# Raw weight halves in the common pool of split weights, and a longer price for loads in the planner

## Chip, core and metric

One NeuronCore of a Trainium2 chip runs the whole program. The metric is the time of one execution on the device in microseconds (us); the median of several runs is compared.

## What is computed

Two layers of an encoder on 256 tokens of width 1024, in float32. Each layer is a half-step SwiGLU, a mixer of two groups of heads, and a second half-step SwiGLU; a norm follows at the end.

```python
def reference(x, ...):
    for l in range(DEPTH):
        x = x + 0.5 * swiglu(rms_norm(x, ffn1_norm[l]), ffn1_w_gate[l], ffn1_w_up[l], ffn1_w_down[l])
        h = rms_norm(x, mix_norm[l])
        proj = h @ w_in[l]
        y_rwkv = rwkv7_group(proj[..., :RWKV_IN], ...)   # delta rule over tokens
        y_ret = retnet_group(proj[..., RWKV_IN:])        # chunk-causal retention
        mixed = jnp.concatenate([y_rwkv, y_ret], axis=-1)
        x = x + mixed @ w_out[l]
        x = x + 0.5 * swiglu(rms_norm(x, ffn2_norm[l]), ffn2_w_gate[l], ffn2_w_up[l], ffn2_w_down[l])
    return rms_norm(x, final_norm)
```

Nearly all the arithmetic is the matrix products with the weights: 166 pieces of 128 x 2048 numbers (1 MB), each of which is used by both token tiles.

## The kernel before

**Tiles and weights.** The 256 tokens are two tiles of 128. A weight piece is handled in two halves of 128 x 1024 (512 KB). `half` loads such a half once, as float32, and splits it into a high part (a ScalarE copy to fp32r, `whi`) and a low part (a VectorE subtraction, `wlo`). `mm3` then makes three matmuls of 512 columns for each 128 x 512 of weights: high by high, high by low, low by high. So a half feeds 6 matmuls for each token tile, 12 in all. The first four halves (EARLY) are loaded and split in two cuts of 512 columns.

**Feed-forward.** `ffn` goes through 11 blocks of 256 columns of gate and up (tile `gu`), makes hh with a ScalarE Silu and a VectorE product, transposes hh on TensorE (`tr`), splits the transposed block into `ht` (ScalarE, then VectorE), and multiplies with the rows of the down weights into `acc`. `norm_T` transposes x and splits it into `parts`.

**Mixer.** `mix` follows PLAN. The delta rule needs the inverse of small triangular blocks; for that, `inverse` sends them through DRAM and back on SyncE's queue (el to d twice, d to mx, mi to d, d to misc, for each tile and layer). `merge` and `chain` are small matmuls that depend on each other.

**Order.** Nothing is emitted as it is written. The calls are recorded as nodes (`record`), priced (`price`), and ordered by a simulated list schedule (`simulate`); `schedule` tries the eight GUIDES with up to SERIES = 4 refinements each and keeps the order with the earliest simulated end. `emit` writes the instructions of all engines in that order, and each engine then runs its own queue in order, waiting at semaphores. The halves' loads are tied to each other in program order (`in_turn`), all on SyncE's queue. A node that needs a new buffer may only start, in the simulation, when enough places of that kind are free.

**Places.** Split halves live in a pool of 22 "wide" places of 4 KB a partition, two for each half, from the first write to the last read. Raw halves live in a ring of three (NRAW, line 31) inside the tile `base`, outside the pool; a load can only be issued when the VectorE split of the half three before has read its buffer. In a profile, `base<-in_w` is such a load, `wide<-base` a ScalarE split, `wide<-base,wide` a VectorE split. All instructions are emitted from one line (L542), so the groups of the profile are told apart by their tiles.

**Price of a load.** A load occupies the simulated fabric for its bytes divided by 290 (in ns), and lands 2000 ns after that.

Of the kernel before, what the change touches and what calls it, by code (L numbers as in the profile page):

```python
# [12 lines left out]
F32 = mybir.dt.float32  # L13
F32R = mybir.dt.float32r
# [6 lines left out]
D = 1024  # L21
S = 256
P = 128
# [4 lines left out]
DEPTH = 2  # L28
RW = 512
HD = 64  # L30
NRAW = 3
XG = (0, 8, 16)
XCUT = (2, 1)
WARM = 1
# [2 lines left out]
FIRST = 2  # L37
# [17 lines left out]
PIECES = 33 + 13 + 4 + 33  # L55
# [6 lines left out]
NBASE = 3072  # L62
# [5 lines left out]
    return ap.unsqueeze(2).to_broadcast(shape)  # L68


PLACES = {"slot": (43, 2048), "wide": (22, 4096), "bank": (8, 2048)}
GUIDES = (5, 7, 10, 14, 20, 25, 30, 40)
SERIES = 4
TURN = -1.0
ENGINES = {"tensor": 0, "vector": 1, "scalar": 2, "gpsimd": 3, "sync": 4}


# [105 lines left out]
class Plan:  # L183
# [178 lines left out]
    def simulate(self, prio):  # L362
# [14 lines left out]
        fabric = 0.0  # L377
# [9 lines left out]
        while done < total:  # L387
            if not events:
                raise Stuck(f"stuck at {t}, {done} of {total}: " + ", ".join(
                    f"{nodes[r[0][1]].ops[0].call} {nodes[r[0][1]].ops[0].args[0].buf.name}" for r in ready if r))  # L390
            t = heapq.heappop(events)
            while events and events[0] <= t:
                heapq.heappop(events)
            while pending and pending[0][0] <= t:
                ft, _, b = heapq.heappop(pending)
                places[b.space].append((ft, b.place))
            for e in range(5):
                if free_at[e] > t:
                    continue
                w, r = waiting[e], ready[e]  # L400
                while w and w[0][0] <= t:
                    i = heapq.heappop(w)[1]
                    heapq.heappush(r, (-prio[i], i))
                held = []
                while r:
                    item = heapq.heappop(r)
                    n = nodes[item[1]]
                    ok = True
                    new = [b for b in n.touched if b.place is None]
                    if new:  # L410
                        wants = {}
                        for b in new:
                            wants[b.space] = wants.get(b.space, 0) + 1
                        if e == 0 and n.dur > 115:
                            wants["bank"] += 1
                        ok = all(len(places[k]) >= v for k, v in wants.items())
                    if ok:
                        break
                    held.append(item)
                else:  # L420
                    n = None
                for h in held:
                    heapq.heappush(r, h)
                if n is None:
                    continue
                for b in new:
                    pool = places[b.space]
                    j = min(range(len(pool)), key=lambda k: pool[k][0])
                    b.place = pool.pop(j)[1]
                    low[b.space] = min(low.get(b.space, 99), len(pool))  # L430
                form = n.ops[0].form
                extra = 0.0
                if e == 0:
                    if state[0] != form:
                        extra = 95.0
                        state[0] = form
                elif e == 2 and form in ("s", "t"):
                    if state[2] != form:
                        extra = 1280.0
                        state[2] = form  # L440
                n.start = t
                dur = n.dur + extra
                n.real = dur
                free_at[e] = t + dur
                heapq.heappush(events, t + dur)
                shift = extra
                if form == "dma":
                    size = n.ops[0].n
                    begin = max(t, fabric)
                    fabric = begin + size / 290.0  # L450
                    land = fabric + 2000.0
                    shift = land - t
                done += 1
                fin = t + dur
                for s, lag in n.succs:
                    a = t + 60 if lag is TURN else t + shift + lag
                    if a > avail[s.i]:
                        avail[s.i] = a
                    need[s.i] -= 1
                    if not need[s.i]:  # L460
                        heapq.heappush(waiting[s.eng], (avail[s.i], s.i))
                        heapq.heappush(events, max(avail[s.i], t))
                if form == "dma":
                    fin = t + shift
                    n.land = shift
                elif e == 0:
                    fin = t + shift + n.ops[-1].at + n.ops[-1].late
                end = max(end, fin)
                for b in n.touched:
                    b.last = max(b.last, fin + 60)  # L470
                    left[b.i] -= 1
                    if not left[b.i]:
                        heapq.heappush(pending, (b.last, b.i, b))
                        heapq.heappush(events, b.last)
# [15 lines left out]
    def schedule(self):  # L490
# [3 lines left out]
        way, n = self.tails(), len(self.nodes)  # L494
        best = None
        for guide in GUIDES:
            prio = [w + guide * (n - i) * 1e5 / n for i, w in enumerate(way)]
            for k in range(SERIES):
                try:
                    end = self.simulate(prio)  # L500
                except Stuck:
                    break
                if best is None or end < best[0]:
                    best = (end, prio)
# [5 lines left out]
    def emit(self, ctx, tc):  # L510
        nc = tc.nc
        sp = ctx.enter_context(tc.tile_pool(name="sbuf", bufs=1))
        pp = ctx.enter_context(tc.tile_pool(name="psum", bufs=1, space=PSUM))
        dp = ctx.enter_context(tc.tile_pool(name="dram", bufs=1, space=bass.MemoryType.DRAM))
        for b in self.bufs:
            if b.space == "fixed":
                b.real = sp.tile(b.shape, b.dt, name=b.name, tag=b.name)
        pools = {"slot": sp, "bank": pp, "dram": dp}
        wide = [sp.tile([P, 1024], F32R, name=f"wide{i}", tag=f"wide{i}") for i in range(PLACES["wide"][0])]

        def place(b):
            size, tag = b.elems, f"{b.name}{b.i}"
            if b.space == "wide":
                b.real = wide[b.place]
                return
            if b.space in PLACES:
                size, tag = PLACES[b.space][1] // SIZE[b.dt], f"{b.space}{b.place}"
            v = pools[b.space].tile([b.shape[0], size], b.dt, name=f"{b.name}_{b.i}", tag=tag, bufs=1)[:, :b.elems]
# [16 lines left out]
VERBOSE = False  # L545


class Trunk:
    def __init__(self, plan, x, w, vecs, lora, fgain, consts, out):
# [1 line left out]
        self.vecs_d, self.lora_d = vecs, lora  # L551
        self.A = self.plan = plan
        self.nc = nc = plan
        base = plan.fixed([P, NBASE + (2 + NRAW) * D], F32, "base")
        parts = plan.fixed([P, NT, 2, KD, P], F32R, "parts")
        self.x, self.xh, self.xl = [], [], []
        for t in range(NT):
# [4 lines left out]
        self.c = base[:, :NBASE]  # L562
        nc.scalar.dma_start(self.c[:, C_ID:C_ID + P], consts[:, C_ID:C_ID + P])
        self.load_x(0)
        self.raw = base[:, NBASE + 2 * D:].rearrange("p (n i) -> p n i", n=NRAW)
        self.nraw = 0
        self.consts_d = consts
        self.scan = self.c[:, C_SCAN:C_SCAN + 256].bitcast(BF16)
        nc.vector.memset(self.scan, 1.0)
# [44 lines left out]
    def half(self, i, h):  # L614

        if (i, h) not in self.wq:
            nc = self.nc
            raw = self.raw[:, self.nraw % NRAW]
            self.nraw += 1
            cut = 512 if 2 * i + h < EARLY else 1024  # L620
            for c in range(0, 1024, cut):
                nc.sync.dma_start(raw[:, c:c + cut], self.w_d[i][:, 1024 * h + c:1024 * h + c + cut])
                nc.in_turn()
            kind = sum(i % PIECES >= b for b in (33, 33 + FIRST, 46, 50)) % 4
            hi = self.A.get([P, 1024], "whi", F32R, kind)
            lo = self.A.get([P, 1024], "wlo", F32R, kind)
            for c in range(0, 1024, cut):
                s = slice(c, c + cut)
                nc.scalar.activation(hi[:, s], raw[:, s], AF.Copy)
# [838 lines left out]
```

## Time and profile before

| | us |
|---|---|
| median of 3 runs (lowest, highest) | 1076.81 (1074.12, 1077.82) |
| the profiled execution | 1078.31 |
| its span, first to last instruction | 1076.3 |
| TensorE busy | 1051.4 |
| VectorE busy | 662.3 |
| ScalarE busy | 598.3 |

The span is what the trace shows; the profiled execution's time has 2.0 us more around it. TensorE's matmuls are pipelined and their ends are modelled, so a busy TensorE is not TensorE at its peak: the same 37 matmuls can fill 8.4 us or 10.3 us. Idle time in front of a group is put down to what ended last before it ("<-").

### The profile page before, as it was taken

The numbers are of one execution on the slowest core, as the hardware profiler recorded it, in microseconds if no ns is written. First come the engines' busy times: TensorE is split into PE (matmuls) and PEld (weight loads), VectorE is DVE, ScalarE is ACT, GpSimd is POOL, SyncE is SP. The second block draws the span as 40 slices with busy tenths as digits, with TensorE's granted clock in tenths as the row PEclk, the third lists the DMA queues.
The fourth block names the chain that finished last, engine by engine and source line by source line (L and its number), as shares of the span: only waits on it lengthen the run. The fifth ranks groups of instructions, "written<-read, shape, count | busy, mean of one in ns | idle before, by whom it ended". The sixth has DMA issues, their size and how long they took to land.

```text
span 1076.3 us, 16094 instructions
## 1 busy us (share of the span) xinstructions
PE 1051.4 (98%) x6253; PEld 855.4 (79%) x6253; DVE 662.3 (62%) x1055; ACT 598.3 (56%) x1016; POOL 37.0 (3%) x44
## 2 busy tenths in 40 slices
PE   8989999999998999999999999999999999999997
PEld 6768888888776888888888788888887778788885
DVE  6666554678778755555465555447887786555542
ACT  6554444585867654453465444448767856454431
POOL 0000000010001000000000000000101010000000
PEclk9999999999999999999999999999999999999999
DMA  7776556433634465555555555564163336655551
GB/s 233 216 227 209 185 180 222 146 118 117 161 90 145 159 209 188 200 177 194 187 185 179 168 187 192 181 216 153 41 174 111 122 120 212 217 164 193 173 157 40
DMA packets 63773, 181.57 MB, mean 169 GB/s; under 512 B 18513, under 2 KB 18897, under 8 KB 63697
## 3 DMA queue, kind: packets, MB, share of 16 engines
q1 hardware_dynamic: 63264, 180.42, 52.3%
q8 instruction: 49, 0.80, 0.3%
q14 instruction: 28, 0.22, 0.1%
q10 hardware_dynamic: 432, 0.13, 0.1%
HBM read 178.17 MB, written 2.36 MB: 168 GB/s over the span
## 4 chain that ended last, share of the span: by engine, by line
PE 77%; DMA 10%; ACT 5%; DVE 5%; issue 2%; ACTq 0%; POOLq 0%; POOL 0%; SPq 0%; DVEq 0%
PE gu L542 48%; PE acc L542 22%; DMA base<-in_w 9%; PE tr L542 5%; ACT wide L542 3%; DVE wide L542 3%; PE ch L542 1%; PE pre L542 1%; DMA mx<-d 0%; ACT parts L542 0%; DMA base<-in_consts 0%; DVE prod L542 0%; ACT lw L542 0%; DMA d<-el 0%; DVE ht L542 0%
## 5 line engine op out<-in xcount | busy, mean ns | idle before, releaser
L542 PE MATMUL gu<-wide,parts 128*128 128x512 f32 (+1 forms) x2784 | 683.8, 395 | 4.8 <-ACT wide L542 2.0
L542 PEld LDWEIGHTS gu<-wide,parts 128*128 128x128 f32 x2784 | 507.9, 189 | 112.5 <-DVE ht L542 4.9
L542 DVE TENSOR_TENSOR wide<-base,wide 128x1024 fp32r<-128x1024 f32 (+1 forms) x336 | 402.3, 1209 | 225.7 <-ACT wide L542 150.6
L542 ACT ACTIVATE wide<-base 128x1024 fp32r<-128x1024 f32 (+1 forms) x336 | 350.4, 1049 | 283.0 <-DMA base<-in_w 115.1
L542 PE MATMUL acc<-wide,ht 128*128 128x512 f32 x1056 | 256.3, 392 | 0.0
L542 PEld LDWEIGHTS acc<-wide,ht 128*128 128x128 f32 x1056 | 196.9, 188 | 41.1
L542 DVE TENSOR_TENSOR ht<-tr,ht 128x256 fp32r<-128x256 f32 x88 | 36.7, 420 | 90.1 <-ACT ht L542 89.9
L542 ACT ACTIVATE hh<-gu,base 128x256 f32<-128x256 f32 x88 | 41.4, 470 | 67.7 <-PE gu L542 67.1
L542 POOL TENSOR_TENSOR base<-base 128x1 f32<-128x1 f32 (+2 forms) x26 | 32.1, 1235 | 983.1 <-DVE base L542 983.1
L542 DVE SCALAR_TENSOR_TENSOR hh<-gu,base,hh 128x256 f32<-128x256 f32 x88 | 42.1, 478 | 8.6 <-ACT hh L542 8.6
L542 PE MATMUL tr<-base,hh 128*128 128x128 f32 x176 | 39.5, 272 | 4.7 <-DVE ht L542 4.7
L542 ACT ACTIVATE ht<-tr 128x256 fp32r<-128x256 f32 x88 | 32.4, 370 | 15.1 <-PE tr L542 14.8
L542 ACT ACTIVATE parts<-tr,base 128x128 fp32r<-128x128 f32 x96 | 30.0, 368 | 17.2 <-PE tr L542 8.8
L542 DVE SCALAR_TENSOR_TENSOR parts<-tr,base,parts 128x128 fp32r<-128x128 f32 x96 | 29.4, 344 | 11.3 <-ACT parts L542 10.6
L542 PEld LDWEIGHTS tr<-base,hh 128*128 128x128 f32 x176 | 24.5, 140 | 14.3 <-DVE ht L542 6.4
L542 ACT ACTIVATE junk<-base 128x1024 bf16<-128x1024 f32 (+1 forms) x16 | 15.3, 956 | 23.6 <-DVE base L542 23.5
L542 DVE SCALAR_TENSOR_TENSOR shd<-tr,base,shd 128x127 f32<-128x127 f32 x56 | 17.3, 343 | 14.1 <-ACT shd L542 13.8
L542 DVE SCALAR_TENSOR_TENSOR base<-acc,base 128x512 f32<-128x512 f32 x16 | 11.0, 686 | 20.6 <-PE acc L542 20.5
L542 PE MATMUL gu<-wide,rh 128*128 128x512 f32 x64 | 23.2, 420 | 0.2 <-DVE base L542 0.2
L542 PE MATMUL gu<-wide,mh 128*128 128x512 f32 x64 | 21.4, 415 | 0.6 <-ACT mh L542 0.6
L542 ACT ACTIVATE shd<-tr,base 128x128 f32<-128x128 f32 x56 | 17.1, 364 | 7.9 <-PE tr L542 5.7
L542 PE MATMUL tr<-base 128*128 128x128 f32 x96 | 16.7, 286 | 1.4 <-DMA base<-in_consts 1.2
(149 smaller groups left out, 590.0 us busy)
## 6 DMA issues: line engine op xcount, KB each, us to landing
base<-in_w SPq DMA_DIRECT2D x328, 512.0 KB, 4.5
base<-in_w SPq DMA_DIRECT2D x8, 256.0 KB, 5.5
lora<-in_lora SPq DMA_DIRECT2D x4, 256.0 KB, 6.1
d<-el SPq DMA_DIRECT2D x8, 128.0 KB, 3.3
out<-ot SPq DMA_DIRECT2D x4, 256.0 KB, 2.2
base<-in_consts SPq DMA_DIRECT2D x1, 805.0 KB, 8.0
base<-in_x SPq DMA_DIRECT2D x2, 256.0 KB, 3.0
base<-in_x SPq DMA_DIRECT2D x1, 512.0 KB, 6.5
```

Source lines behind the costliest of these rows:

```text
L542: getattr(getattr(nc, op.eng), op.call)(*args, **kw)
```

## The change

The ring of three raw buffers is removed, and a raw half becomes a buffer of the pool ("wide", `kind = "w"`), like the high and the low part. The pool has 25 places instead of 22, so the memory is the same. A raw half takes its place when its load is issued and gives it back after its splits. In the simulation, a SyncE node that needs a wide place must leave SPARE = 3 others free, a ScalarE one must leave one other free, a VectorE one none. A load now occupies the fabric for bytes / 400 and lands 2700 + bytes / 480 ns after that. In `emit`, the 22 wide tiles were made once, before the instructions; now a wide place is made anew at each use, like the places of the other pools.

```diff
--- before.py
+++ after.py
@@ -28,7 +28,6 @@
 DEPTH = 2
 RW = 512
 HD = 64
-NRAW = 3
 XG = (0, 8, 16)
 XCUT = (2, 1)
 WARM = 1
@@ -68,10 +67,11 @@
     return ap.unsqueeze(2).to_broadcast(shape)
 
 
-PLACES = {"slot": (43, 2048), "wide": (22, 4096), "bank": (8, 2048)}
+PLACES = {"slot": (43, 2048), "wide": (25, 4096), "bank": (8, 2048)}
 GUIDES = (5, 7, 10, 14, 20, 25, 30, 40)
 SERIES = 4
 TURN = -1.0
+SPARE = 3
 ENGINES = {"tensor": 0, "vector": 1, "scalar": 2, "gpsimd": 3, "sync": 4}
 
 
@@ -413,6 +413,8 @@
                             wants[b.space] = wants.get(b.space, 0) + 1
                         if e == 0 and n.dur > 115:
                             wants["bank"] += 1
+                        if "wide" in wants:
+                            wants["wide"] += (0, 0, 1, 0, SPARE)[e]
                         ok = all(len(places[k]) >= v for k, v in wants.items())
                     if ok:
                         break
@@ -447,8 +449,8 @@
                 if form == "dma":
                     size = n.ops[0].n
                     begin = max(t, fabric)
-                    fabric = begin + size / 290.0
-                    land = fabric + 2000.0
+                    fabric = begin + size / 400.0
+                    land = fabric + 2700.0 + size / 480.0
                     shift = land - t
                 done += 1
                 fin = t + dur
@@ -498,7 +500,9 @@
             for k in range(SERIES):
                 try:
                     end = self.simulate(prio)
-                except Stuck:
+                except Stuck as ex:
+                    if VERBOSE:
+                        print(ex)
                     break
                 if best is None or end < best[0]:
                     best = (end, prio)
@@ -515,14 +519,10 @@
         for b in self.bufs:
             if b.space == "fixed":
                 b.real = sp.tile(b.shape, b.dt, name=b.name, tag=b.name)
-        pools = {"slot": sp, "bank": pp, "dram": dp}
-        wide = [sp.tile([P, 1024], F32R, name=f"wide{i}", tag=f"wide{i}") for i in range(PLACES["wide"][0])]
+        pools = {"slot": sp, "wide": sp, "bank": pp, "dram": dp}
 
         def place(b):
             size, tag = b.elems, f"{b.name}{b.i}"
-            if b.space == "wide":
-                b.real = wide[b.place]
-                return
             if b.space in PLACES:
                 size, tag = PLACES[b.space][1] // SIZE[b.dt], f"{b.space}{b.place}"
             v = pools[b.space].tile([b.shape[0], size], b.dt, name=f"{b.name}_{b.i}", tag=tag, bufs=1)[:, :b.elems]
@@ -551,7 +551,7 @@
         self.vecs_d, self.lora_d = vecs, lora
         self.A = self.plan = plan
         self.nc = nc = plan
-        base = plan.fixed([P, NBASE + (2 + NRAW) * D], F32, "base")
+        base = plan.fixed([P, NBASE + 2 * D], F32, "base")
         parts = plan.fixed([P, NT, 2, KD, P], F32R, "parts")
         self.x, self.xh, self.xl = [], [], []
         for t in range(NT):
@@ -562,8 +562,6 @@
         self.c = base[:, :NBASE]
         nc.scalar.dma_start(self.c[:, C_ID:C_ID + P], consts[:, C_ID:C_ID + P])
         self.load_x(0)
-        self.raw = base[:, NBASE + 2 * D:].rearrange("p (n i) -> p n i", n=NRAW)
-        self.nraw = 0
         self.consts_d = consts
         self.scan = self.c[:, C_SCAN:C_SCAN + 256].bitcast(BF16)
         nc.vector.memset(self.scan, 1.0)
@@ -615,15 +613,14 @@
 
         if (i, h) not in self.wq:
             nc = self.nc
-            raw = self.raw[:, self.nraw % NRAW]
-            self.nraw += 1
+            kind = "w"
+            raw = self.A.get([P, 1024], "raw", F32, kind)
+            hi = self.A.get([P, 1024], "whi", F32R, kind)
+            lo = self.A.get([P, 1024], "wlo", F32R, kind)
             cut = 512 if 2 * i + h < EARLY else 1024
             for c in range(0, 1024, cut):
                 nc.sync.dma_start(raw[:, c:c + cut], self.w_d[i][:, 1024 * h + c:1024 * h + c + cut])
                 nc.in_turn()
-            kind = sum(i % PIECES >= b for b in (33, 33 + FIRST, 46, 50)) % 4
-            hi = self.A.get([P, 1024], "whi", F32R, kind)
-            lo = self.A.get([P, 1024], "wlo", F32R, kind)
             for c in range(0, 1024, cut):
                 s = slice(c, c + cut)
                 nc.scalar.activation(hi[:, s], raw[:, s], AF.Copy)
```

## Rows read from the trace of the kernel before

**Rows 1.** The page, part 1: engine, busy us, share of the span, instructions

```profile
PE 1051.4 (98%) x6253; PEld 855.4 (79%) x6253; DVE 662.3 (62%) x1055; ACT 598.3 (56%) x1016; POOL 37.0 (3%) x44
```

**Rows 2.** Windows: start:end, length, busy of each engine, granted clock, DMA share, GB/s

```profile
54.00:81.00 27.00, 23.69 (x100) 18.60 (x99) 16.64 (x21) 15.34 (x21) 0.00 (x0) 0.94 0.71 228
...
75.00:86.00 11.00, 11.00 (x44) 8.82 (x44) 6.66 (x9) 4.31 (x7) 0.00 (x0) 0.84 0.78 270
...
324.00:351.00 27.00, 24.19 (x340) 18.54 (x335) 22.94 (x38) 21.62 (x44) 4.20 (x2) 1.00 0.46 141
594.00:621.00 27.00, 26.10 (x118) 20.90 (x117) 14.88 (x19) 11.73 (x17) 0.00 (x0) 1.00 0.56 181
918.00:945.00 27.00, 25.39 (x115) 20.26 (x114) 15.80 (x20) 14.88 (x22) 0.00 (x0) 1.00 0.56 191
```

**Rows 3.** The chain that ended last, 60 to 97 us: start, length, what

```profile
60.53 4.21 DMA base<-in_w
64.83 1.07 ACT wide L542
65.92 1.23 DVE wide L542
67.17 4.80 DMA base<-in_w
...
88.48 8.41 PE gu L542 x37
```

**Rows 4.** Timeline, 70 to 86 us: start, length, instruction, idle before and its releaser

```profile
70.19 1.06 ACT L542 ACTIVATE wide<-base 128x1024 fp32r<-128x1024 f32 x1 [1.91 <-DMA base<-in_w]
71.16 0.46 ACT L542 ACTIVATE hh<-gu,base 128x256 f32<-128x256 f32 x1
...
72.06 1.06 ACT L542 ACTIVATE wide<-base 128x1024 fp32r<-128x1024 f32 x1 [0.44 <-DMA base<-in_w]
72.43 0.48 DVE L542 SCALAR_TENSOR_TENSOR hh<-gu,base,hh 128x256 f32<-128x256 f32 x1
73.02 0.37 ACT L542 ACTIVATE ht<-tr 128x256 fp32r<-128x256 f32 x1
...
74.29 0.42 DVE L542 TENSOR_TENSOR ht<-tr,ht 128x256 fp32r<-128x256 f32 x1
...
74.76 0.33 PE L542 MATMUL tr<-base,hh 128*128 128x128 f32 x1 [2.86 <-DVE ht L542]
...
75.19 10.30 PE L542 MATMUL gu<-wide,parts 128*128 128x512 f32 x37
```

**Rows 5.** Timeline, 609 to 613 us, and one transpose at 928.81

```profile
609.42 1.06 ACT L542 ACTIVATE wide<-base 128x1024 fp32r<-128x1024 f32 x1 [2.96 <-DMA base<-in_w]
...
612.12 0.44 PE L542 MATMUL tr<-base,hh 128*128 128x128 f32 x2 [0.49 <-DVE ht L542]
...
928.81 0.33 PE L542 MATMUL tr<-base,hh 128*128 128x128 f32 x1 [0.80 <-DVE ht L542]
```

**Rows 6.** Timeline, 345 to 348 us, the start of the second feed-forward of layer 0

```profile
345.53 1.06 ACT L542 ACTIVATE wide<-base 128x1024 fp32r<-128x1024 f32 x1 [0.88 <-DMA base<-in_w]
...
347.04 1.20 PE L542 MATMUL gu<-wide,parts 128*128 128x512 f32 x4 [0.51 <-ACT parts L542]
```

**Rows 7.** Waits, whole run: engine, tile, waited for: us in total, times, longest

```profile
ACT wide L542 <- DMA base<-in_w: 115.1, 118, 3.0
```

**Rows 8.** DMA issues: tiles, queue, count, KB each, median us to landing

```profile
base<-in_w SPq DMA_DIRECT2D x328, 512.0 KB, 4.5
...
base<-in_x SPq DMA_DIRECT2D x1, 512.0 KB, 6.5
```

**Rows 9.** Windows, the first loads (columns as in rows 2)

```profile
3.00:9.00 6.00, 2.89 (x12) 1.61 (x10) 1.68 (x8) 2.59 (x8) 0.00 (x0) 1.00 0.99 294
```

**Rows 10.** The chain that ended last, mixer of layer 1: start, length, what

```profile
798.61 5.03 DMA mx<-d
```

**Rows 11.** Timeline of TensorE, end of the mixer of layer 0

```profile
339.28 1.08 PE L542 MATMUL ch<-uv,lq 64*64 64x64 f32 x16 [1.33 <-ACT uv L542]
```

## Prediction

> **What bounds the kernel now.** I read the engine shares of the page first. TensorE is busy 98% of the span [rows 1], so almost nothing can be won from work that lies beside it; a gain has to come out of the few places where TensorE stands still or runs slowly. Next I read the span in windows of 27 us to find those places. In most windows TensorE is busy for all 27.00 us. The exceptions away from the first and last microseconds are in [rows 2]: 23.69 of 27 in 54:81, 24.19 in 324:351, 26.10 in 594:621 and 25.39 in 918:945.
>
> Then I asked the chain of waits and the timeline what ended each stall. In the opening the chain is a closed ring: a load of half a weight piece (4.21 us), its split on ScalarE (1.07) and on VectorE (1.23), and then the next load (4.80), which may only be issued when that split has freed one of the three raw buffers [rows 3]. One turn, start of load to start of load, takes 67.17 − 60.53 = 6.64 us. The stall follows from queues that run in order. ScalarE stands at two splits for loads that haven't landed (1.91 and 0.44 us), with an hh and an ht activation queued behind them; VectorE finishes ht at 74.71, and TensorE, whose queue holds the transpose that has to follow that ht, waits 2.86 us [rows 4]. Afterwards 37 matmuls take 10.30 us where 37 a little later take 8.41 [rows 3, 4], and the granted clock averages 0.84 in 75:86 [rows 2] (its levels are 1.2 and 2.4 GHz).
>
> The other stalls have the same shape: at 609.42 ScalarE has waited 2.96 us for a load, and ht and the transpose come late [rows 5]. In the whole run ScalarE waits for weights 118 times, 115.1 us together [rows 7]; nearly all of that costs nothing, since TensorE has split weights in hand. Only where hh or ht stands behind it does TensorE pay.
>
> **The change part by part.** No arithmetic is removed: the same 336 halves are loaded, split and multiplied, and the memory is the same (22 + 3 places become 25). What changes is who may hold a place, and the order that the planner writes.
>
> (1) *The ring of three goes.* A load needs four free places (one and the spare three), a ScalarE split two, a VectorE split one. So at the start 22 loads can be issued without waiting for a split, and the ring's turn of 6.64 us no longer sets the supply.
>
> (2) *Loads are priced longer.* A lone 512 KB load was taken as 524,288/290 + 2000 = 3.8 us, less than the measured median of 4.5 [rows 8]; now it is 1.31 + 2.70 + 1.09 = 5.1 us, more than measured. A split that is placed behind a load then meets data that is there, and hh and ht behind it aren't held.
>
> What both can win is the stalls that such waits end:
> - 54:81: 27.00 − 23.69 = 3.31 us idle, and 10.30 − 8.41 = 1.89 us of slow clock after it: 5.2 us.
> - 594:621: 27.00 − 26.10 = 0.9 us. 918:945: 27.00 − 25.39 = 1.6 us, half of it the 0.80 at 928.81 [rows 5].
> - 347.04: 0.5 us, where a split that waited 0.88 us for its load stands before the activations of the next norm [rows 6].
>
> Together 8.2 us. The rest of 324:351 is not counted: there a chain of small matmuls waits for ScalarE [rows 11], which no load releases.
>
> What is given back:
>
> (3) *Loads are believed to stream too fast.* The new price puts 524,288/400 = 1.31 us between loads in a burst. With the DMA engines 0.99 busy they moved 294 GB/s [rows 9], which is 1.78 us a half. Splits are taken as early as the planner can. Twelve matmuls of a half last 12 × 8.41/37 = 2.73 us [rows 3], so four halves take 10.9 us; VectorE has two hh (0.48) and two ht (0.42) in that time [rows 4] and room for (10.9 − 1.8)/1.23 = 7.4 splits, one in 1.47 us. Over the 18 loads that follow the first few, the order runs ahead of the data by up to 18 × (1.78 − 1.47) = 5.6 us, and ScalarE would again stand at loads with hh behind. The bounds are 0 and 5.6 us. I take 1.5, nearer the low end, because loads that land before the first place is freed give a head start, and the pool of split halves grows meanwhile. The Trainium skill, "DMA: Bandwidth & Descriptors", section "Specifications", gives a limit of about 358 GB/s from HBM for a core. By it a half lands every 1.46 us, an estimate, the order never runs ahead, and the sum would come out 1.5 us lower; the trace disagrees with its 294 GB/s at full engines.
>
> (4) *Few split pairs at first.* With 22 raw halves in 25 places, three are left. Two halves can be split (each takes two places and gives one back), and the third must wait until both token tiles have used the first. Until tile 1 begins, whose x takes 6.5 us to land [rows 8], tile 0 then has only the 2 × 6 matmuls of two halves, 2.7 us of work. Cost: between −1 us (tile 1 starts earlier, fewer splits stand before its norm) and +2.7 us; I take 0.5.
>
> (5) *Waits that move.* A load now waits on SyncE's queue for matmuls that free a place, instead of for VectorE's last split. Behind it in that queue stand later loads and, in the mixer, the relays through DRAM (el to d, d to mx, mi to d, d to misc), and VectorE waits for these. What hides it is other matrix work beside the mixer; where that runs out, it is exposed (first rival). I cost it at nothing, with bounds 0 and what the rival gives.
>
> (6) *A new order everywhere.* All engines get new positions. In the mixer the bound on either side is the idle of the tail window, 27.00 − 24.19 = 2.81 us a layer [rows 2], so ±5.6 us over two layers. I take 0.
>
> Sum against the profiled execution (1078.3 us: span 1076.3 and 2.0 around it): 1078.3 − 8.2 + 1.5 + 0.5 = 1072.1. That execution is 1.5 us over the median of the runs, so the forecast in terms of the median is **1070.6 us**, 0.6% less.
>
> **The rivals.**
> - *Slower: relays held on SyncE.* A load that waits for a place holds every DMA behind it. Matmuls free a pair of places every 2.73 us. If half of the eight relay steps of the late tile (four a layer) are each held for one such interval, and the chain has nothing beside it, that is 4 × 2.73 = 10.9 us, and 1070.6 + 10.9 = 1081.5. It decides from the point where TensorE has no other matmuls left, as at 339.28, where it already waits 1.33 us inside the chain [rows 11]. For it: one relay load is on the chain with 5.03 us [rows 10]. Against it: this relay is the early tile's, and TensorE kept busy. The Trainium skill, "DMA: Bandwidth & Descriptors", section "Queues, rings and completion order", says that each DMA engine consumes descriptors in ring order; by it a relay would also queue behind loads already issued, 1.78 us for each, and no row here separates that from the issue wait.
> - *No change: the opening gives all of it back.* Terms 3 and 4 at their upper ends, 5.6 and 2.7: 1070.6 + 4.1 + 2.2 = 1076.9. For it: today's stall is itself an order that trusts loads too much, and a burst price of 1.31 us trusts them more than 1.81 did. Against: raw halves already loaded make late splits harmless for the matmuls themselves.
> - *It does not do what it says after the opening.* Splits get places before loads, so the pool fills with pairs, a load is issued only when nothing is left to split, and ScalarE meets it at landing as before. Then only the 5.2 us of the opening are won, less 2.0: 1076.8 − 3.2 = 1073.6. For it: four places against two. Against: the price of 5.1 us covers the measured 4.5.
> - *More than forecast.* In the mixer a landed raw half takes one place, not two, so more weights wait there, and the new order also closes the tail windows: 1070.6 − 5.6 = 1065.0.
>
> **How the numbers follow.** Forecast 0.41, slower rival 0.14, no change 0.20, not what it says 0.13, more 0.12. A difference under 0.3% (3.2 us) is about what can't be told from no change here. Faster by more than that, below 1073.6: 0.41 + 0.12 + half of 0.13, 0.59. Within: 0.20 + 0.07 = 0.27. Slower: 0.14. The range is 1063 to 1081: the low end lets the larger gain come out 2 us better, the high end takes in "no change" with its spread and the edge of the slower rival, whose longer tail, and the last bit of the low side, make up the 0.2 left out.
>
> **What would show it.** Right: 54:81 has TensorE busy for 27 us at a granted clock of 1.00; ScalarE's waits for weights fall from 115 us to under 40; SyncE's waits name matmuls in place of VectorE's splits; loads in the first 30 us run at about 290 GB/s. Term 3 is there if ScalarE still waits for loads between 18 and 45 us and TensorE waits for ht there. Term 4 shows as idle TensorE between 9 and 17 us. The slower rival shows as relay DMAs issued late after a load that waits for matmuls, and as longer idle in the chain of the later tile. The forecast is wrong if the stalls of 594:621 and 918:945 come back at other places with DMA as their releaser, or if new idle in the mixer exceeds 3 us a layer.

## The result, and the profile after

| | before | after |
|---|---|---|
| median of 4 runs each, taken together (us) | 1076.94 | 1059.96 |
| lowest, highest | 1074.12, 1077.82 | 1059.41, 1060.45 |
| the profiled execution | 1078.31 | 1060.01 |
| its span | 1076.3 | 1058.2 |

The ratio of the means is 0.9847, with a 95% interval of 0.9828 to 0.9865. By the medians it is 17.0 us less, where the forecast took 6.2 (1076.8 to 1070.6). The direction was right; the time lies below the low end of the range, 1063.

First the page of the kernel after: the engines' busy times, and the chain that ended last, as shares of the span.

```profile
PE 1043.3 (99%) x6253; PEld 854.1 (81%) x6253; DVE 668.7 (63%) x1055; ACT 593.9 (56%) x1016; POOL 37.7 (4%) x44
...
PE 98%; DMA 1%; ACT 0%; issue 0%; DVE 0%; ACTq 0%; POOLq 0%; POOL 0%
```

TensorE is busy for 8 us less than in [rows 1] and covers 98% of the chain of waits. Before it covered 77%, and the chain went through DMA, ScalarE and VectorE again and again, as [rows 3] shows for the opening. Then the windows, with the columns of [rows 2]: the first three are the opening, the last four those of [rows 2].

```profile
3.00:9.00 6.00, 3.34 (x12) 1.87 (x10) 1.77 (x8) 2.69 (x8) 0.00 (x0) 1.00 0.95 301
9.00:17.00 8.00, 8.00 (x27) 5.92 (x27) 4.22 (x13) 4.83 (x14) 0.56 (x1) 1.00 1.03 412
54.00:81.00 27.00, 27.00 (x126) 22.27 (x125) 16.51 (x20) 12.45 (x19) 0.00 (x0) 1.00 0.61 212
...
324.00:351.00 27.00, 25.90 (x211) 20.49 (x210) 22.57 (x39) 13.05 (x27) 5.12 (x3) 1.00 0.18 55
594.00:621.00 27.00, 27.00 (x124) 22.19 (x124) 15.77 (x20) 12.71 (x19) 0.00 (x0) 1.00 0.55 179
918.00:945.00 27.00, 27.00 (x126) 22.14 (x125) 13.97 (x19) 13.01 (x20) 0.00 (x0) 1.00 0.54 189
```

The three stalls of [rows 2] in the feed-forwards are gone: 27.00 busy at a granted clock of 1.00. The window 9:17 has no idle TensorE, and its loads ran at 412 GB/s. Next the waits (engine, tile, releaser: us in total, times, longest): ScalarE for loads, the longest one of TensorE, and SyncE's queue.

```profile
ACT whi L542 <- DMA raw<-in_w: 29.4, 18, 4.6
...
PE gu L542 <- ACT whi L542: 2.7, 1, 2.7
...
SPq L542 <- PE gu L542: 455.2, 121, 19.4
SPq L542 <- DVE wlo L542: 163.6, 53, 26.6
SPq L542 <- PE acc L542: 161.9, 42, 10.6
```

ScalarE waits 18 times for loads in place of the 118 of [rows 7], and TensorE's list has no wait for hh or ht. Before, the first two of these lines stood in TensorE's list, and the third headed SyncE's:

```profile
PE tr L542 <- DVE ht L542: 4.7, 4, 2.9
...
PE gu L542 <- DVE ht L542: 1.7, 3, 0.8
...
SPq L542 <- DVE wide L542: 663.7, 257, 21.2
```

**Where the 18.1 us of span went.** TensorE is idle for 24.9 us of the span before and 14.9 after, so 10.0 us are idle time and 8.1 are busy time. Fixed windows don't compare once the kernels have shifted, so I cut both traces where equal amounts of matrix work were done, each matmul weighted with the usual time of its shape. The cuts are good to about 1 us. In brackets is what the lower granted clock took: the time spent at it, times (1 − clock).

```
            opening       1st FFN rest   mixer 0   middle FFNs   mixer 1       last FFN, end
before      103.6 (1.7)   105.4          160.7     347.1         161.5 (1.7)   198.0 (1.8)
after        97.3         105.5          157.5     344.5         158.1         195.2 (1.3)
difference   -6.3          +0.1           -3.2      -2.6          -3.4          -2.8
```

So 6.3 us come from the opening, 2.6 from the two middle feed-forwards, 2.8 from the last feed-forward and the end, and 6.6 from the mixers, for which the forecast had taken 0.5 (the wait at 347.04 [rows 6] lies in the stage of mixer 0). The 176 transposes of hh, matched by their number in both traces where only a feed-forward runs, give a second measure: 7.2 us in the opening, 2.1 in the middle, 3.3 at the end.

### The profile page after: what moved, and what is told of

The parts are those of the page before. It is cut to its first block, busy times and chain, and to the rows that moved or that the text cites. A ratio compares the mean times of both kernels' runs of the same rounds, so it can differ in the third digit from the quotient of the medians.

```text
span 1058.2 us, 16001 instructions
## 1 busy us (share of the span) xinstructions
PE 1043.3 (99%) x6253; PEld 854.1 (81%) x6253; DVE 668.7 (63%) x1055; ACT 593.9 (56%) x1016; POOL 37.7 (4%) x44
## 4 chain that ended last, share of the span: by engine, by line
PE 98%; DMA 1%; ACT 0%; issue 0%; DVE 0%; ACTq 0%; POOLq 0%; POOL 0%
PE gu L542 64%; PE acc L542 22%; PE tr L542 7%; PE ch L542 2%; PE pre L542 2%; DMA base<-in_vecs 1%; DVE base L542 0%; ACT x L542 0%; DVE g L542 0%; ACT parts L542 0%; ACTq L542 0%; ACT junk L542 0%; ACT ot L542 0%; DVE tc L542 0%; ACT mh L542 0%
## 5 line engine op out<-in xcount | busy, mean ns | idle before, releaser
L542 PE MATMUL gu<-whi,parts 128*128 128x512 f32 (+1 forms) x1856 | 586.2, 395 | 3.3 <-ACT whi L542 2.7
L542 DVE TENSOR_TENSOR wlo<-raw,whi 128x1024 fp32r<-128x1024 f32 (+1 forms) x336 | 401.6, 1209 | 147.0 <-ACT whi L542 77.9
L542 ACT ACTIVATE whi<-raw 128x1024 fp32r<-128x1024 f32 (+1 forms) x336 | 343.4, 1046 | 114.7 <-PE acc L542 47.3
L542 PEld LDWEIGHTS gu<-whi,parts 128*128 128x128 f32 x1856 | 346.2, 189 | 74.5 <-ACT whi L542 3.1
L542 PE MATMUL gu<-wlo,parts 128*128 128x512 f32 (+1 forms) x928 | 352.0, 392 | 0.0
L542 PE MATMUL acc<-whi,ht 128*128 128x512 f32 x704 | 222.0, 393 | 0.0
L542 PEld LDWEIGHTS gu<-wlo,parts 128*128 128x128 f32 x928 | 175.2, 189 | 34.0 <-DVE wlo L542 0.4
L542 PEld LDWEIGHTS acc<-whi,ht 128*128 128x128 f32 x704 | 131.8, 188 | 27.7
L542 PE MATMUL acc<-wlo,ht 128*128 128x512 f32 x352 | 133.3, 391 | 0.0
L542 PEld LDWEIGHTS acc<-wlo,ht 128*128 128x128 f32 x352 | 66.1, 188 | 13.7
```

The source lines that it names most:

```text
L542: getattr(getattr(nc, op.eng), op.call)(*args, **kw)
```

## The experiments

The change has two halves, the places and the price, and it writes a new order besides. The theories that the expectations letter: A, that of the prediction, has the ring set the supply in the opening; D has a price below the measured landing place splits where they must stand, with hh and ht behind them; F has only the shared pool help; G has the mixers lose to the granted clock after a short idle stretch; C has the orders scatter, and the change a lucky one; K and L divide the mixers' gain between order and change. All kernels compute the whole reference. The stages quoted are those of the table above, from each kernel's own trace.

**Price alone, ring kept.**

```diff
-                    fabric = begin + size / 290.0
-                    land = fabric + 2000.0
+                    fabric = begin + size / 400.0
+                    land = fabric + 2700.0 + size / 480.0
```

> The ring of three stays; only the planner's price of a load changes (bytes/400, then 2700 + bytes/480). Theory A (two causes): the price alone ends the stalls in which ScalarE holds hh or ht behind a split whose load has not landed, about 4 us in the feed-forwards, and about 6 us of lost time at the ends of the mixers, while the opening, which the ring limits, keeps its 7 us: 1066 to 1069 us. Rival B (the ring is the cause everywhere): loads come no earlier, so the waits only move in the order: 1074 to 1078 us. Rival C (a lucky order): anything from 1064 to 1082 us, with the mixers moved and the feed-forwards not.

Measured 1061.02 us, ratio 0.9844 [0.9808, 0.9879], as much as the whole change and below what all three theories expected. The opening takes 95.5 us with the ring of three still there. Its waits of ScalarE for loads and two of its windows:

```profile
ACT wide L542 <- DMA base<-in_w: 51.9, 60, 2.3
...
54.00:81.00 27.00, 27.00 (x127) 22.32 (x126) 16.95 (x21) 14.11 (x21) 0.00 (x0) 1.00 0.64 208
...
918.00:945.00 27.00, 27.00 (x125) 22.22 (x124) 16.90 (x21) 14.07 (x21) 0.00 (x0) 1.00 0.63 208
```

A ring that set the supply would have kept the stall of [rows 4] whatever the price. It is gone, so theory A falls for the opening: the order made the stall.

**Places alone.** The changed kernel with the old price:

```diff
-                    fabric = begin + size / 400.0
-                    land = fabric + 2700.0 + size / 480.0
+                    fabric = begin + size / 290.0
+                    land = fabric + 2000.0
```

> Raw halves take places of the pool; the price of a load is the old one (bytes/290, then 2000). Theory A: the opening wins its 7 us, since 22 loads go out at once; splits are again planned at 3.8 us after the issue against 4.5 measured, so the stalls of the feed-forwards and of the mixers stay: 1068 to 1071 us. Rival B (the pool is the cause everywhere): 1060 to 1063 us, with ScalarE waiting less than 40 us for loads. Rival C: no pattern by stage.

Measured 1065.26, ratio 0.988 [0.985, 0.9909], between what A and B expected. TensorE never waits for hh or ht here either, and ScalarE waits 22.8 us for loads; opening 98.5, middle feed-forwards 344.5. Either half alone ends the stalls, and together they bring little more than one. Here a load is priced at 3.8 us and its median landing is 4.8, so a price below the landing isn't enough for a stall.

**Price taken apart.** Three kernels: the changed kernel with the old streaming (`size / 290`) and the new latency; the kernel before with the new latency alone; and the kernel before with the new streaming alone, a lone load at 1.31 + 2.0 = 3.3 us.

```diff
# the changed kernel, slow stream
-                    fabric = begin + size / 400.0
+                    fabric = begin + size / 290.0
# the kernel before, latency alone
-                    land = fabric + 2000.0
+                    land = fabric + 2700.0 + size / 480.0
# the kernel before, stream alone
-                    fabric = begin + size / 290.0
+                    fabric = begin + size / 400.0
```

> The changed kernel, with the stream priced at bytes/290 and the long landing kept. In the changed kernel's opening 512 KB loads moved at 409 to 412 GB/s, 1.28 us each, against 1.31 priced. Theory A: a stream that is believed slower only delays early splits, of which there are enough: 1059 to 1062 us. Rival (the right stream price is part of the gain): the order of the opening holds splits back and TensorE waits there, 1063 to 1067 us.

Measured 1068.71, ratio 0.9916 [0.9886, 0.9947]. That is slower than either theory expected. Opening and middle hardly move (97.4 and 345.0), so the rival's wait in the opening isn't there. Of the 8.1 us that its trace is longer than that of the changed kernel, 4.3 are in mixer 1 (3.4 of them clock) and 2.3 in mixer 0.

> Ring of three as before; only the landing of a load is priced longer (bytes/290, then 2700 + bytes/480: 5.6 us for a lone 512 KB load, where 4.5 is measured in the kernel before). The run with the whole new price in the kernel before gave 1061.0 us. Theory D (data that are there when their split's turn comes): the longer landing is the cause, 1060 to 1064 us, and no transposes wait for ht. Rival E (a stream that is believed faster lets more splits be placed early): the landing alone wins less than half, 1069 us or more.

Measured 1075.95 over 10 runs, ratio 0.9992 [0.9964, 1.0021]: no gain as a whole, as E had it. Yet the feed-forwards are cured, as D had it (opening 96.7, middle 344.8, no wait for hh or ht). Mixer 0 gives most of it back, 168.4 us with 10.2 in clock. Two windows inside it:

```profile
296.00:300.00 4.00, 2.80 (x75) 1.78 (x73) 3.75 (x13) 3.92 (x15) 0.00 (x0) 0.90 0.79 256
300.00:312.00 12.00, 12.00 (x165) 8.57 (x166) 7.95 (x26) 6.69 (x13) 2.01 (x3) 0.50 0.22 60
```

TensorE idles 1.2 us of 4, then runs 12 us at a granted clock of 0.50, the lower of its two levels (1.2 GHz). The clock isn't the whole loss: the fastest of the ten executions had a mean clock of 0.995 and still took 1070.46 us, 9.4 more than the whole new price.

> Ring of three as before; only the stream is priced faster (bytes/400, then 2000: 3.3 us for a lone 512 KB load, further below the measured 4.5). Theory D: splits are planned before their data are there even more often, 1077 to 1084 us, with ScalarE waiting more than 115 us for loads. Rival E: 1061 to 1069 us. Rival C (lucky orders): no relation between the price and the time.

Measured 1091.13, ratio 1.013 [1.0082, 1.0177], slower. ScalarE's waits for loads, TensorE's waits, and the window of the opening:

```profile
ACT wide L542 <- DMA base<-in_w: 234.2, 179, 3.7
...
PE tr L542 <- DVE hh L542: 6.4, 5, 2.9
PE gu L542 <- DVE ht L542: 3.3, 3, 1.7
...
PE acc L542 <- DVE hh L542: 2.4, 2, 2.1
PE acc L542 <- DVE ht L542: 2.1, 1, 2.1
...
54.00:81.00 27.00, 24.07 (x109) 18.97 (x108) 18.46 (x25) 15.58 (x22) 0.00 (x0) 1.00 0.64 211
```

Here the price is further below the 4.5 us of [rows 8], and the stalls multiply: TensorE waits 14.2 us for hh and ht, and the middle feed-forwards take 353.0 (the profiled execution, 1096.16 us, is the longest of four; the shortest took 1084.19). The direction and ScalarE's waits are those of theory D; the loss is larger than the 1077 to 1084 us that it expected. Rival E falls.

**Sharing, or more raw buffers?** The kernel before with the same memory divided otherwise:

```diff
-NRAW = 3
+NRAW = 5
-PLACES = {"slot": (43, 2048), "wide": (22, 4096), "bank": (8, 2048)}
+PLACES = {"slot": (43, 2048), "wide": (20, 4096), "bank": (8, 2048)}
```

> The kernel before with a ring of five raw buffers and 20 places for split halves, same memory, old price. Theory D: what counts is that data have landed when their split's turn comes, and deeper loads do that as well as a longer price: the transposes stop waiting for ht, the opening wins 4 to 7 us, 1066 to 1072 us. Rival F (only sharing the pool helps, since a ring is bound to its own order): 1074 to 1078 us.

Measured 1062.99, ratio 0.9885 [0.9866, 0.9904], 3 us below the range of theory D. ScalarE's waits for loads and the one wait left for hh or ht:

```profile
ACT wide L542 <- DMA base<-in_w: 17.7, 18, 4.5
...
PE tr L542 <- DVE hh L542: 0.5, 1, 0.5
```

Theory F falls: five raw buffers with 20 places do nearly all of it at the old price. With the kernel of the places alone, this is the second in which loads are issued earlier and a price that is too low does no harm.

**The reserve.** The changed kernel with `SPARE = 8`:

```diff
-SPARE = 3
+SPARE = 8
```

> The changed kernel with eight places kept free of loads instead of three, so 17 loads at once in the opening and five pairs that can be split before the first is freed. Theory D: supply is not what bounds, the feed-forwards stay as they are, 1058 to 1064 us, with differences in the mixers only. Rival (few pairs at first cost the changed kernel something): the opening is 1 to 3 us shorter.

Measured 1070.83, ratio 0.9957 [0.9941, 0.9974]. Opening and middle stay at 96.7 and 345.1; the mixers take 162.8 and 162.9, 10.1 us more than after. So theory D's range is missed, by the mixers that it left open, and the rival falls: with more places for split pairs the opening is 0.6 us shorter at most (96.7 against 97.3), within the accuracy of the cuts.

**How much is the order's luck?** Every run so far is also another order. So I gave the kernels other GUIDES (the guesses from which the planner starts), the same for each pair, first for the kernel before, the changed one and the price alone:

```diff
-GUIDES = (5, 7, 10, 14, 20, 25, 30, 40)
+GUIDES = (6, 8, 12, 17, 22, 28, 35, 45)
```

> The kernel before with eight other guides (6, 8, 12, 17, 22, 28, 35, 45), so another order at the same prices and places. Theory A: the limits are the same, the time stays within 2.5 us of 1076.9, and the opening loses as much. Rival C (orders scatter, and the change had a lucky one): the time differs by more than 5 us, in the mixers.

Measured 1074.8 over 10 runs, ratio 0.9982 [0.9957, 1.0006]. The time is the one that theory A expected, but the opening loses less, 99.0 us in place of 103.6.

> The changed kernel with eight other guides (6, 8, 12, 17, 22, 28, 35, 45). Theory D: the gain does not hang on one order, 1057 to 1064 us. Rival C: 1066 us or more, most of it in the mixers.

Measured 1065.79, ratio 0.9924 [0.9891, 0.9958], just outside the range of D and just short of C's.

> Ring of three, whole new price, eight other guides. Theory D: within 4 us of the 1061.0 us that the new price gave with the old guides. Rival C: 1067 us or more.

Measured 1068.29, ratio 0.9924 [0.9903, 0.9945], which is what rival C expected.

About half of the gain is gone with these guides. Of that, 4.4 us went in the opening, and not because the changed kernel lost there: its opening is 97.1 us (95.8 with the price alone), but that of the kernel before is itself shorter, 99.0. So three more pairs, one execution each:

```diff
# pair C
+GUIDES = (4, 9, 11, 16, 18, 23, 33, 50)
# pair D
+GUIDES = (3, 13, 15, 19, 24, 27, 32, 37)
# pair E
+GUIDES = (6.5, 8.5, 9.5, 12.5, 16.5, 21, 31, 45)
```

> The kernel before with guides (4, 9, 11, 16, 18, 23, 33, 50). Theory K (only the feed-forwards belong to the change, the mixers go with the order): opening and middle feed-forwards 98 to 104 and 347 to 349 us, the two mixers together anywhere from 314 to 326 us. Rival L (the mixers belong to the change too): the two mixers together 320 to 325 us, as in the kernel before (321.9).

> The changed kernel with the same guides as the run before it. Theory K: opening 96 to 97 us and middle feed-forwards 344 to 346 us, no transposes waiting for ht, the two mixers together anywhere from 314 to 326 us. Rival L: the two mixers together 313 to 318 us, as in the changed kernel (315.3).

> The kernel before with guides (3, 13, 15, 19, 24, 27, 32, 37). Theory K: opening and middle feed-forwards 98 to 104 and 347 to 349 us, mixers together anywhere from 314 to 326 us. Rival L: mixers 320 to 325 us.

> The changed kernel with the same guides as the run before it. Theory K: opening 96 to 97 us, middle feed-forwards 344 to 346 us, mixers together anywhere from 314 to 326 us. Rival L: mixers 313 to 318 us.

> The kernel before with guides (6.5, 8.5, 9.5, 12.5, 16.5, 21, 31, 45), a fifth order. So far four orders of it gave 1065.8 to 1083.3 us. Theory K: opening above 98 us with transposes waiting for ht, mixers less their clock loss 319 to 322 us. Rival (no part of the change survives another order): opening 96 to 97 us and the whole below 1066 us.

> The changed kernel with the same guides, a fifth order. So far four orders gave 1060.0 to 1065.8 us. Theory K: opening 96 to 97 us, no transposes waiting for ht, mixers less their clock loss 315 to 320 us, 1058 to 1066 us. Rival: 1068 us or more.

The five pairs, the shipped guides first (medians where there are several runs):

```
                 shipped    B        C        D        E       mean
kernel before    1076.9   1074.8   1083.3   1065.8   1071.6   1074.5
changed kernel   1060.0   1065.8   1064.6   1063.9   1066.6   1064.2
stage means      opening  1st FFN rest  mixer 0  middle  mixer 1  last FFN, end
kernel before    100.3    106.0         159.5    347.0   162.5    198.0
changed kernel    96.6    105.5         157.8    345.1   161.9    195.4
```

The changed kernel is faster in all five, by 1.9 to 18.6 us, 10.3 in the mean. Five differences that scatter so leave that mean uncertain by 3.3 us (its standard error), and single executions add to it: the ten of the kernel before with guides B run from 1071.78 to 1080.68 us. So the 1.9 us of pair D alone show nothing. The opening is shorter in every pair. In mixer 0 the two just touch (158.1 to 160.7 against 157.5 to 158.3); in mixer 1 they overlap (159.3 to 168.4 against 158.1 to 165.8). For the two mixers together, rival L's ranges fail in all four kernels of pairs C and D (328.0, 318.7, 318.8 and 320.0 us), in the second by less than the cuts are good for; K's fails only in the first, which lost 8.5 us to the clock. Less the clock, the mixers take 319.0 us before and 317.0 after in the mean of five orders, with ranges that overlap (318.0 to 320.5, 315.6 to 319.0). K's other misses are small: the middle feed-forwards of the kernel before in pair D (344.7), its mixers less the clock in pair E (318.0), and the whole of the changed kernel there (1066.6).

Order D of the kernel before shows that the total of waiting isn't what counts: ScalarE waits 136.2 us for loads, more than in [rows 7], and TensorE pays 1.8.

```profile
ACT wide L542 <- DMA base<-in_w: 136.2, 130, 3.0
...
PE gu L542 <- DVE ht L542: 1.8, 1, 1.8
```

In the changed kernel's five orders TensorE never waits for hh or ht; in the other five it does, for 1.8 to 6.4 us.

**Filling the mixer.** Theory G on the latency-alone order: two extra bf16 matmuls ahead of the first write of each small bank of `merge` and `chain`. They are overwritten. The lines that hand over `scan` and `flat` are left out here:

```diff
+FILL = 2
...
+                            if v.buf.name in ("pre", "ch") and op.call == "matmul" and op.kw["rhs"].dt == F32 and v.buf.elems <= 256:
+                                scan = self.scan.ap()
+                                for _ in range(FILL):
+                                    nc.tensor.matmul(v.buf.flat, lhsT=scan[:, :P], rhs=scan[:, :v.buf.elems],
+                                                     start=True, stop=True)
```

> The kernel of the longer landing alone (1075.95 us), order unchanged, with two extra bf16 matmuls of at most 256 columns ahead of each first write of a small bank of merge and chain, so that TensorE does something while it waits there. If no idle took them up they would cost at most 9.6 us. Theory G (its loss against the whole new price is the lower clock in the mixers, 0.50 granted in 300:312 after 1.2 us of idle): the clock in that stretch returns to 1.00 and the time falls to 1064 to 1073 us. Rival H (the order itself is longer there): 1078 to 1086 us.

Measured 1082.96, ratio 1.0061 [1.0039, 1.0083]. The window at 300, a GpSimd operation of this kernel and the matmuls held behind it, then the same operation of the latency-alone kernel (start, duration, engine, tile, wait before it):

```profile
300.00:312.00 12.00, 10.89 (x244) 7.60 (x244) 10.53 (x35) 10.78 (x28) 1.94 (x3) 1.00 0.39 135
...
241.43 6.44 POOL L549 TENSOR_TENSOR base<-base 128x8 f32<-128x8 f32 x1 [10.26 <-DVE base L549]
...
248.58 0.75 PE L549 MATMUL tr<-base,sq 128*128 128x128 f32 x4 [2.62 <-ACT sq L549]
```

```profile
241.45 1.76 POOL L542 TENSOR_TENSOR base<-base 128x8 f32<-128x8 f32 x1 [10.28 <-DVE base L542]
```

The time lies in rival H's range, not in theory G's. The clock did come back: it is 1.00 here, and the matmuls of 296:312 (the order is the same, so they can be matched one by one) took 12.2 us in place of 16.0. But that doesn't show that the fillers brought it back. The idle time was hardly filled (0.97 us in 300:304, where the same work stands now, against 1.20 in 296:300), and the whole stretch came 4.3 us later. That delay began at 241, where the GpSimd operation took 4.7 us longer; ScalarE and then TensorE waited behind it. Its length isn't the fillers' doing as far as can be seen: among the 160 operations of this kind in the 20 traces, two took more than 4 us, this one and one of 4.37 in the kernel with `SPARE = 8`. Mixer 1 took 4.5 us longer too, for which no cause is known.

**A first load moved.** In the changed kernel, layer 0's vectors are loaded behind the identity:

```diff
+        self.first = plan.nodes[-1]
...
+        if l == 0:
+            nc.behind(self.first)
```

> The changed kernel with the load of the identity ahead of the load of the vectors on ScalarE's queue, as the order of the ring with the new price had it, where the transposes of x began at 3.91 us instead of about 5.1. Theory: the opening is 1.2 us shorter and the rest as before, 1057 to 1060 us. Rival C: the new order moves the mixers by more than that, either way.

Measured 1058.64, ratio 0.9844 [0.9828, 0.986], the lowest median here, but not a gain: the kernel after has a ratio of 0.9847. The reason given was wrong, since the changed kernel already issues the identity first. The edit changed no order: every engine works through the same sequence of tiles as in the kernel after, and SyncE and ScalarE issue the same loads. So this is a second measurement of the kernel after, and 1.3 us is what two such measurements differ by.

## Why the prediction was right and wrong

From the profiled execution of before to that of after it is 18.3 us, 12 more than forecast: about 6 of them are in the mixers (step 6), 4 in the feed-forwards (step 2), and 2 are steps 3 and 4, which took off what was never lost. None of the signs named for a wrong forecast showed; the miss is all on the fast side.

- **What bounds the kernel: right.** The stalls of [rows 4] and [rows 5] are hh and ht held behind splits whose loads hadn't landed, and they vanish, to 0.5 us at most, in the kernels whose loads are priced above the measured 4.5 us of [rows 8] or issued earlier. The lower price of the stream-alone kernel brings more of them. (The halves are 332, not 336: 336 is the count of splits, with four halves split in two cuts.)
- **Step 1, the ring: wrong as a cause.** The price alone keeps the ring and gains as much. The turn of 6.64 us was the pace of an order, not a limit. The chain of waits names the buffer as releaser because the order used it so; whether another order was possible it can't say.
- **Step 2: right in kind, too small.** By matched transposes the opening won 7.2 us against 5.2; the stretch with the stall of 594:621 won 1.5 against 0.9, and that with the stall of 918:945 2.1 against 1.6. One reason is a stall that I left out: the window 27:54 is an exception as well, and [rows 2] lack it. The other is that matmuls also run further apart around a stall, without an idle gap in the profile. The lines below are of before: the window, then rows of TensorE's timeline. A block of 256 columns, for both token tiles, takes 11.39 us undisturbed (from 85.33 to 96.72). The block from 57.09 took 12.12, of which 0.45 is idle; that from 33.50 took 12.19, with 0.56 idle; and that from 69.21, with the stall of [rows 4], 16.12.

```profile
27.00:54.00 27.00, 26.44 (x121) 21.36 (x120) 16.30 (x20) 14.26 (x20) 0.00 (x0) 1.00 0.71 218
...
33.50 0.27 PE L542 MATMUL tr<-base,hh 128*128 128x128 f32 x1
...
36.74 0.33 PE L542 MATMUL tr<-base,hh 128*128 128x128 f32 x1 [0.56 <-DVE ht L542]
...
45.69 0.28 PE L542 MATMUL tr<-base,hh 128*128 128x128 f32 x1
...
57.09 0.27 PE L542 MATMUL tr<-base,hh 128*128 128x128 f32 x1
...
63.86 5.52 PE L542 MATMUL gu<-wide,parts 128*128 128x512 f32 x23 [0.45 <-DVE ht L542]
...
69.21 0.28 PE L542 MATMUL tr<-base,hh 128*128 128x128 f32 x1
...
85.33 0.27 PE L542 MATMUL tr<-base,hh 128*128 128x128 f32 x1
...
96.72 0.27 PE L542 MATMUL tr<-base,hh 128*128 128x128 f32 x1
```

- **Step 3: wrong, and with it 1.5 us.** [rows 9] measure the first loads, most of them cuts of 512 columns. The full halves that follow ran at 412 GB/s, 524,288/412 = 1.27 us each, against the price of 1.31 and my 1.78. The order didn't run ahead of the data: ScalarE's first wait for a load in the kernel after is the one below, at 160.92 us. The Trainium skill, "DMA: Bandwidth & Descriptors", section "Specifications", has a limit of about 358 GB/s from HBM for a core; by it the order keeps up, and it did, but the measured 412 is above that limit.

```profile
160.92 1.06 ACT L542 ACTIVATE whi<-raw 128x1024 fp32r<-128x1024 f32 x1 [4.58 <-DMA raw<-in_w]
```

- **Step 4: nil instead of 0.5.** 9:17 has no idle, and a reserve of 8 changes nothing there.
- **Step 5: right at nothing.** SyncE's waits do name matmuls now, 163 times in the two largest groups, against 53 times for VectorE's splits. No relay was held up by a load that waits for matmuls: in the kernel after all 20 were issued within 0.7 us of the end of the operation or transfer whose result they pass on, 18 of them within 0.15. So the slower rival fails at its first step.
- **Step 6, the order taken at 0: the largest miss.** The mixers gave 6.6 us in this pair, beyond the bound of 5.6. That bound was one tail window of mixer 0, doubled. Mixer 1 has losses of its own, which [rows 2] leave out: 27.00 − 25.86 = 1.14 us idle and then a lower clock, in these windows of before.

```profile
837.00:864.00 27.00, 25.86 (x545) 19.80 (x544) 20.41 (x36) 22.20 (x45) 2.54 (x1) 1.00 0.38 122
864.00:891.00 27.00, 26.59 (x144) 21.03 (x145) 21.05 (x39) 15.94 (x33) 3.27 (x3) 0.94 0.46 139
```

How much of it belongs to the change, the five pairs say only roughly: 1.7 us in mixer 0 and 0.7 in mixer 1, the latter within its scatter. Of the 17 us about 10 belong to the change, give or take 3; the rest is that the shipped order of before lies 2.4 us above its mean and that of after 4.2 below its own, which is luck. For mixer 0 a cause can be named but isn't proved: in the five orders of before ScalarE waits there 3.6 to 11.4 us for loads, in the changed ones 0.2 at most. What scatters mixer 1 is partly clock (up to 8.5 us in order C of before); the rest stays open.

In the mean of the five pairs the feed-forwards gave 8.7 us, and the mechanism's terms are 8.2 with steps 3 and 4 at nothing: that part was nearly right. The rival "more than forecast" came nearest (1065.0): as it had it, the rest of the gain is in the mixers; whether for its reason, more landed weights waiting there, no run shows.

## What to carry to other kernels

A static order of in-order engines is only as good as its prices. Price a load at or above the measured time from issue to landing: in the feed-forwards of the latency-alone kernel 5.6 us for a measured 4.3 cost next to nothing, while a split that meets no data holds all that is queued behind it. Or issue loads early enough that the price doesn't matter. This cures that one wait; it doesn't make the whole faster by itself, as the latency-alone kernel shows. A releaser in the chain of waits names what came last in this order, not a limit; change the suspected cost alone before you believe it. Where every edit rewrites the whole order, compare several orders of both kernels before you put a number on an edit, and make sure that the edit changed the order at all.

## What was not expected of the hardware

- Loads of 512 KB ran at 412 GB/s with the DMA engines at 1.03 in 9:17, the first, smaller cuts at 301 with a share of 0.95 in 3:9. The shorter rows of those cuts would explain it; no run separated that.
- Executions of one program differed by 12 us with the clock: the latency-alone kernel took 1070.46 at a mean granted clock of 0.995 and 1082.00 at 0.984; 1075 × 0.011 = 11.8. The clock isn't always the reason: the kernel before with guides B took 1071.78 at 0.997 and 1080.68 at 0.995, where 1075 × 0.002 is 2.
- 1.2 us of idle TensorE were followed by 12 us at 0.50 in the same kernel. In the kernel before, a wait of 1.33 us [rows 11] stands in a window at 1.00.
- The same GpSimd operation on 128 x 8 numbers took 1.76 us in one execution and 6.44 in another kernel's; the profile's spans on GpSimd are rough.
